# First sums of the down projection written by ScalarE, residual kept in the output, final sums added by GpSimd's DMAs

## The chip, the core and the metric

The kernel runs on one core of a Trainium2 chip. A core has TensorE (PE) for matrix products, VectorE (DVE) and ScalarE (ACT) for elementwise work, GpSimd (POOL) and SyncE (SP), each with its own queue of instructions that it works off in order. They meet only at semaphores: an instruction waits until those it depends on have reported. Data lies in the chip's DRAM, in on-chip SBUF of 128 partitions, and in PSUM, into which TensorE writes and from which VectorE and ScalarE read. DMA transfers between DRAM and SBUF are issued here by SP, later in part by GpSimd; 16 DMA engines carry them out. The metric is the device time of one execution in microseconds.

## The reference

One decoder block on 1024 tokens of width 1024. Two token mixers come first; what matters here is the end:

```python
        x = x + y @ w_out[l]
        xn2 = rmsnorm(x, norm2_g[l])
        x = x + jnp.square(jax.nn.relu(xn2 @ w_up[l])) @ w_down[l]
```

`w_up` is 1024 x 4096 and `w_down` is 4096 x 1024, all float32. The `x` of the first line, the residual, is needed twice: for the norm, and to be added to the result of the last line.

## The kernel before, in words

Every float32 operand is split into a high part and a low part (`split`, lines 318 to 320: ScalarE copies into the high part, VectorE subtracts it from the source for the low part), and a product is three matmuls: high by high, high by low, low by high. The large products use a scheme of seven instead of eight sub-products (N1 to N7), whose operands are sums of quarters of the matrices.

**Residual (lines 1040 to 1083).** For each of eight row blocks and two column halves TensorE forms `y @ w_out`, VectorE adds x, and SP stores the sum in `y_d`, a DRAM tile (line 1075). In the second half the first half of a row block is read back from `y_d` for the norm (line 1052).

**Up projection (`product`, `result`, `put_operand`).** Sixteen column units; the squared ReLU is turned into the operands of the down projection, split and stored in the DRAM tile `h_d` (line 1130, `h_d<-hs`).

**Down projection (`down`, lines 1155 to 1181).** The work is 32 blocks u = (c, t): eight chunks c of 512 of the 4096 hidden columns, and within each chunk four t; a block works on the row blocks t and t + 4. A block takes seven products of six 128x512 matmuls. Its rows of `h_d` come as two loads, `xh` and `xl` (`load_rows`, line 1146), into one of three places that rotate with u. The products go to three PSUM banks of a block:

- "a" (a tile `mm`): N1, which ScalarE copies with its sign turned into bank "b" (line 1172), then N2 on top of it;
- "b" (a tile `ms`): N6, N7, N4 one on top of the other;
- "d" (a tile `mm`): N5, then N3 on top of it.

After each product other than N1 VectorE adds or subtracts the bank into half of a row tile `Y[r]` of 128x1024 (line 1177). TensorE may put the next product on a bank only when the read before it is done: (u, N7) waits until N6's sum in "b" is read, (u, N4) until N7's is. `Y[0]` to `Y[7]` stay in SBUF over all chunks. They start from the residual: `load_sums` (line 1149) loads them from `y_d`, Y0 and Y4 early (line 1099), the other six when the up projection has ended (lines 1203 to 1205). In the last chunk SP stores each finished half to `out` (line 1179).

**Weights (class `Weights`).** Chunks of `w_down` come as four tiles `raw` (line 176), from which VectorE forms sums (line 153) and `split` makes the seven operands. Those of chunk 1 are called y1a, y1b, y1c, wh3/wl3, w1a, w1b and w1c, with h or l for the high and the low part.

**Order.** TensorE's order is written out by hand (main loop, lines 1216 to 1221): N6 and N5 of block u, N1 of u + 1, N7 of u, N2 of u + 1, N3 and N4 of u. The other engines' order is set by the scheduler of the framework from the order of the program and its own estimate of times. An instruction that waits holds up all that stands behind it on its engine.

Of the kernel before, what the change touches and what calls it, by code (L numbers as in the profile page):

```python
# [10 lines left out]
F = mybir.dt.float32  # L11
R = mybir.dt.float32r
AF = mybir.ActivationFunctionType
OP = mybir.AluOpType
# [255 lines left out]
def hybrid_block(ctx: ExitStack, tc: tile.TileContext, a: dict, out: bass.AP):  # L270
# [24 lines left out]
    v_d = dram.tile([HEADS, S, DH], F, name="v_d")  # L295

    h_d = dram.tile([FF // 512, 2, 4, P, 7, 2, P], F, name="h_d")
    y_d = dram.tile([S, D], F, name="y_d")

    def slot_of(from_):  # L300

# [699 lines left out]
    with ExitStack() as ph:  # L1001
# [41 lines left out]
        def load_rows(n):  # L1043

            nb, t = order[n]
            ts = slice(t * P, (t + 1) * P)
            xt = pn.tile([P, 512], F, name="xr")
            nc.sync.dma_start(xt, a["x"][ts, halves()[nb]])
            y0 = None
            if nb == 1:  # L1050
                y0 = pn.tile([P, 512], F, name="y0")
                nc.sync.dma_start(y0, y_d[ts, :512])
            ahead.append((xt, y0))

        load_rows(0)
        for nb in range(2):
            us = W.take(4)
            ns = halves()[nb]
            for n, t in enumerate([t for b, t in order if b == nb]):
# [12 lines left out]
                y = xt  # L1072
                nc.vector.tensor_tensor(y, pm, xt, op=OP.add)
                nc.scalar.activation(pm, y, AF.Square, accum_out=ssq[:, t, nb:nb + 1])
                nc.sync.dma_start(y_d[ts, ns], y)
                if nb == 1:
                    nc.vector.tensor_tensor(ssq[:, t, 2:3], ssq[:, t, 0:1], ssq[:, t, 1:2], op=OP.add)
                    rsqrt(ssq[:, t, 3:4], ssq[:, t, 2:3], 1.0 / D)
# [9 lines left out]
    with ExitStack() as ph:  # L1088
# [3 lines left out]
        def temps():  # L1092

            nonlocal up_pool
            if up_pool is None:
                assert pipe.slot > last_turn
                norm2.close()
                y0 = pool(sumst, "y0", 1)
                load_sums(0, [y0.tile([P, D], F, name=f"Y{r}") for r in (0, 4)])
                up_pool = pool(ph, "p26", 2)  # L1100
            return up_pool

# [43 lines left out]
                    nc.sync.dma_start(x.bitcast(F), h_d[c, i, t].rearrange("p o k q -> p (o k q)"))  # L1146
                    rows[u].append(x.rearrange("p (o k q) -> p o k q", o=7, k=2))

        def load_sums(t, places):

            for r, place in zip((t, t + 4), places):
                Y[r] = place
                nc.sync.dma_start(place, y_d[r * P:(r + 1) * P, :])

        def down(u, name):

            c, t = units[u]
            b = sums.setdefault(u, {})
            bank = BANK[name]
            fresh = bank not in b  # L1160
            if fresh:
                b[bank] = mm.tile([P, 512], F, name="mm")
            o = DOWN.index(name)
            wh, wl = W["dn", c, name]
            xh, xl = rows[u]
            pipe.step(b[bank], [(xh[:, o, k], xl[:, o, k], wh[:, 512 * k:512 * k + 512], wl[:, 512 * k:512 * k + 512])
                                for k in range(2)], None, fresh)
            ps = b[bank]
            lo, hi = halves()
            if name == "N1":  # L1170
                b["b"] = ms.tile([P, 512], F, name="ms")
                nc.scalar.activation(b["b"], ps, AF.Copy, scale=-1.0)  # L1172
            else:
                r, ns, op, last = {"N2": (t, lo, OP.add, True), "N6": (t, hi, OP.subtract, False),
                                   "N5": (t + 4, hi, OP.subtract, False), "N7": (t + 4, hi, OP.add, True),
                                   "N3": (t, hi, OP.add, True), "N4": (t + 4, lo, OP.add, True)}[name]
                nc.vector.tensor_tensor(Y[r][:, ns], Y[r][:, ns], ps, op=op)  # L1177
                if last and c == NC - 1:
                    nc.sync.dma_start(out[r * P:(r + 1) * P, ns], Y[r][:, ns])
            if t == 3:  # L1180
                W.free(("dn", c, name))

# [17 lines left out]
        exts.close()  # L1200
        y1 = pool(sumst, "y1", 1, "right")

        places = {t: [y1.tile([P, D], F, name=f"Y{r}") for r in (t, t + 4)] for t in (1, 3, 2)}
        for t in range(1, 4):
            load_sums(t, places[t])
        for x in "abc":
            W.places["y1" + x] = [y1.tile([P, UW], R, name=f"y1{x}{i}") for i in "hl"]
        W.free(("place", "y1"))
# [113 lines left out]
```

## Time and profile before

| | |
|---|---|
| median of 3 runs | 2300.4 us (2299.05 to 2302.49) |
| the profiled execution | 2299.8 us |
| its span, first to last instruction | 2297.7 us |
| PE matmul busy | 2236.2 us (97%) |
| DVE, ACT, POOL busy | 1341.9, 988.0, 103.0 us |
| SP's DMA queue | 351.63 MB, 48.3% of 16 engines |

The up projection's last units and the start of the down projection lie between about 1900 and 2015 us; the down projection then runs to the end. A row of the profile gives engine, source line, operation and output <- inputs; "L1177 DVE TENSOR_TENSOR Y<-Y,ms" is VectorE adding the bank "b" into Y. In rows of a timeline the first two numbers are start and duration in us, and a bracket gives the idle time before and what ended it. "SPq" rows are SP's issues of transfers, whose data lands later. In the table by stretch of time a DMA share near 1 means that all 16 engines are carrying data.

### The profile page before, as it was taken

To read this page: it belongs to the slowest core of one execution; us is meant where nothing else is said; L and a number is where in the kernel's file an instruction comes from. 1 tells how busy PE (TensorE), PEld (TensorE's weight loads), DVE (VectorE), ACT (ScalarE), POOL (GpSimd) and SP (SyncE) were. 2 spreads that over 40 slices of the span, in tenths; PEclk is the share of its full clock that TensorE was granted. 3 is DMA by queue.
4 is the path that set the end of the run, shared out by engine and by line. 5 is a ranking of instruction groups with operands and counts; after the bars stand their busy time and mean duration, and the time that the engine had idled before them with its cause. 6 is when DMAs were issued, how large, how long until landed. Compare 5 with 4: busy or idle time off the path is not lost.

```text
span 2297.7 us, 29975 instructions
## 1 busy us (share of the span) xinstructions
PE 2236.2 (97%) x10868; PEld 1915.5 (83%) x10868; DVE 1341.9 (58%) x2588; ACT 988.0 (43%) x2166; POOL 103.0 (4%) x148
## 2 busy tenths in 40 slices
PE   8999999999999999989999999999999999699999
PEld 7999999998888888878888778888787777588887
DVE  6444545455544445548777842453877778777774
ACT  5444435345443333435555533122666667422220
POOL 1111111110000000000000000000000000000000
PEclk9999999999999999999999999999999999899999
DMA  4313132223233333363433484554377789966655
GB/s 146 97 52 114 53 93 93 81 84 101 88 110 110 110 110 110 106 174 111 120 119 101 140 289 152 170 179 142 115 219 230 229 238 277 329 241 261 234 223 201
DMA packets 288805, 353.53 MB, mean 154 GB/s; under 512 B 14609, under 2 KB 215441, under 8 KB 288658
## 3 DMA queue, kind: packets, MB, share of 16 engines
q1 hardware_dynamic: 288658, 351.63, 48.3%
q8 instruction: 85, 1.39, 0.3%
q14 instruction: 62, 0.51, 0.1%
HBM read 229.84 MB, written 121.73 MB: 153 GB/s over the span
## 4 chain that ended last, share of the span: by engine, by line
PE 77%; DVE 8%; DMA 7%; ACT 4%; issue 3%; POOL 0%; SPq 0%; POOLq 0%; ACTq 0%; DVEq 0%
PE mm L223 51%; PE ms L223 20%; DMA raw<-in_w_up 3%; ACT wh L319 2%; DVE wl L320 2%; DMA h_d<-hs 1%; PE ms L605 1%; DVE hs L320 1%; PE ms L585 1%; DVE raw L121 1%; PE tr L661 1%; DVE xl L320 1%; PE ms L598 1%; PE ms L821 1%; DVE u L1120 1%
## 5 line engine op out<-in xcount | busy, mean ns | idle before, releaser
L223 PE MATMUL mm<-wh,xh 128*128 128x384 f32 (+1 forms) x1280 | 503.8, 394 | 0.0
L320 DVE TENSOR_TENSOR wl<-raw,wh 128x1024 fp32r<-128x1024 f32 (+2 forms) x274 | 297.4, 1088 | 298.6 <-ACT wh L319 295.5
L223 PE MATMUL mm<-wh,xl 128*128 128x384 f32 (+1 forms) x1280 | 460.4, 360 | 4.3 <-DVE xl L320 3.2
L223 PE MATMUL mm<-wl,xh 128*128 128x384 f32 (+1 forms) x1280 | 459.2, 359 | 0.0
L319 ACT ACTIVATE wh<-raw 128x1024 fp32r<-128x1024 f32 (+2 forms) x274 | 257.6, 949 | 301.0 <-PE mm L223 77.9
L223 PE MATMUL mm<-xl,wh 128*128 128x512 f32 x848 | 310.0, 390 | 1.7 <-DVE xl L320 1.7
L223 PE MATMUL mm<-xh,wh 128*128 128x512 f32 x848 | 310.5, 391 | 0.0
L223 PE MATMUL mm<-xh,wl 128*128 128x512 f32 x720 | 280.7, 390 | 0.0
L223 PEld LDWEIGHTS mm<-wh,xl 128*128 128x128 f32 x1280 | 241.4, 189 | 27.2 <-DVE xl L320 4.3
L223 PEld LDWEIGHTS mm<-wh,xh 128*128 128x128 f32 x1280 | 242.6, 190 | 21.0 <-ACT ms L1172 0.5
L223 PEld LDWEIGHTS mm<-wl,xh 128*128 128x128 f32 x1280 | 243.4, 190 | 19.1
L223 PE MATMUL ms<-xh,wh 128*128 128x512 f32 x604 | 239.8, 397 | 16.8 <-ACT u L393 13.8
L223 PE MATMUL ms<-xh,wl 128*128 128x512 f32 x604 | 236.0, 391 | 0.0
L223 PE MATMUL ms<-xl,wh 128*128 128x512 f32 x604 | 235.9, 391 | 0.0
L223 PEld LDWEIGHTS mm<-xl,wh 128*128 128x128 f32 x848 | 159.7, 188 | 35.1 <-DVE xl L320 2.1
L223 PEld LDWEIGHTS mm<-xh,wh 128*128 128x128 f32 x848 | 159.7, 188 | 34.0 <-ACT u L396 0.7
L223 PEld LDWEIGHTS mm<-xh,wl 128*128 128x128 f32 x720 | 135.6, 188 | 28.2
L223 PEld LDWEIGHTS ms<-xh,wh 128*128 128x128 f32 x604 | 113.8, 188 | 45.1 <-ACT u L393 18.8
L223 PEld LDWEIGHTS ms<-xh,wl 128*128 128x128 f32 x604 | 113.7, 188 | 24.0
L223 PEld LDWEIGHTS ms<-xl,wh 128*128 128x128 f32 x604 | 113.8, 188 | 22.3
L592 ACT ACTIVATE pr<-s,acc 128x128 f32<-128x128 f32 (+1 forms) x96 | 43.1, 449 | 148.4 <-DVE acc L590 125.5
L1177 DVE TENSOR_TENSOR Y<-Y,ms 128x512 f32<-128x512 f32 x96 | 65.8, 685 | 62.2 <-PE ms L223 62.1
(254 smaller groups left out, 3284.2 us busy)
## 6 DMA issues: line engine op xcount, KB each, us to landing
h_d<-hs SPq DMA_DIRECT2D x112, 512.0 KB, 5.7
xh<-h_d SPq DMA_DIRECT2D x32, 896.0 KB, 5.9
xl<-h_d SPq DMA_DIRECT2D x32, 896.0 KB, 7.2
raw<-in_w_att SPq DMA_DIRECT2D x48, 384.0 KB, 4.0
raw<-in_w_up SPq DMA_DIRECT2D x32, 512.0 KB, 5.1
raw<-in_w_down SPq DMA_DIRECT2D x32, 512.0 KB, 6.0
sg_d<-sg SPq DMA_DIRECT2D x32, 256.0 KB, 2.1
raw<-in_w_rqk_q SPq DMA_DIRECT2D x16, 512.0 KB, 3.7
```

Of the source, the lines that this page charges most:

```text
L121: self.nc.vector.tensor_tensor(x, x, y, op=OP.add)
L223: self.nc.tensor.matmul(ps, x, y, start=start, stop=stop, skip_group_check=not first)
L319: nc.scalar.activation(dst_h, src, AF.Copy)
L320: nc.vector.tensor_tensor(dst_l, src, dst_h.bitcast(F), op=OP.subtract)
L585: nc.tensor.matmul(sp[:, :n], qT[:, b * P:(b + 1) * P], kT[:, k0:k0 + n], start=True, stop=True)
L592: nc.scalar.activation(st["p"][:, :n], s[:, :n], AF.Exp, bias=acc[:, b, DH:DH + 1], accum_out=acc[:, b, DH + 1:DH + 2])
L598: nc.tensor.transpose(tp[:, j * P:(j + 1) * P], st["p"][:, j * P:(j + 1) * P], ident)
L605: nc.tensor.matmul(po[:, :DH], st["t"][:, j * P:(j + 1) * P], V[:, k0 // P + j, :], start=(j == 0), stop=(j == nk - 1))
L661: nc.tensor.transpose(pt[:, j, :], qk[:, j, :], ident)
L821: nc.tensor.matmul(sp[:, :P], kT[:, f], qT[:, f], start=(f == 0), stop=(f == 1))
L1120: nc.vector.tensor_tensor(held[j, x], held[j, x], held[j, y], op=OP.add)
L1177: nc.vector.tensor_tensor(Y[r][:, ns], Y[r][:, ns], ps, op=op)
```

## The change

The residual is stored in `out` itself instead of `y_d`, and read back from there for the norm. The eight loads of Y are gone: Y starts as the first sum of chunk 0. In each half of a row tile the first product that reaches it (N2, N6, N5 and N4 of chunk 0) is written by ScalarE, with the sign as its scale; N7 and N3 of chunk 0 and everything of later chunks are added by VectorE as before. At the end each finished half of Y is sent by GpSimd with a DMA that adds it to what is in `out`.

```diff
-    y_d = dram.tile([S, D], F, name="y_d")
...
-                nc.sync.dma_start(y0, y_d[ts, :512])
+                nc.sync.dma_start(y0, out[ts, :512])
...
-                nc.sync.dma_start(y_d[ts, ns], y)
+                nc.sync.dma_start(out[ts, ns], y)
...
-                load_sums(0, [y0.tile([P, D], F, name=f"Y{r}") for r in (0, 4)])
+                Y.update({r: y0.tile([P, D], F, name=f"Y{r}") for r in (0, 4)})
...
-        def load_sums(t, places):
-
-            for r, place in zip((t, t + 4), places):
-                Y[r] = place
-                nc.sync.dma_start(place, y_d[r * P:(r + 1) * P, :])
...
-                nc.vector.tensor_tensor(Y[r][:, ns], Y[r][:, ns], ps, op=op)
+                begun = c > 0 or name in ("N7", "N3")
+                if not begun:
+                    nc.scalar.activation(Y[r][:, ns], ps, AF.Copy, scale=1.0 if op == OP.add else -1.0)
+                else:
+                    nc.vector.tensor_tensor(Y[r][:, ns], Y[r][:, ns], ps, op=op)
                 if last and c == NC - 1:
-                    nc.sync.dma_start(out[r * P:(r + 1) * P, ns], Y[r][:, ns])
+                    nc.gpsimd.dma_start(out[r * P:(r + 1) * P, ns], Y[r][:, ns], accum_op=OP.add)
...
-        places = {t: [y1.tile([P, D], F, name=f"Y{r}") for r in (t, t + 4)] for t in (1, 3, 2)}
-        for t in range(1, 4):
-            load_sums(t, places[t])
+        Y.update({r: y1.tile([P, D], F, name=f"Y{r}") for t in (1, 3, 2) for r in (t, t + 4)})
```

TensorE's order of matmuls stays as it is. The other engines' orders move around the first blocks of the down projection. Three places follow, each with the rows of the program before and then of the changed one. The number behind a tile's name is that of its buffer; line numbers of the changed program are a few lower, apart from 1172, which is the copy of N1 before and the write of a first sum after.

On **VectorE**, where chunk 1's weights are made, before. Bank "b" of block 1 is ms_17791, and its N6 sum is the last row but one.

```order
L320 TENSOR_TENSOR y1bl_17728<-raw1_17703,y1bh_17727 128x1024
L320 TENSOR_TENSOR y1cl_17730<-raw2_17705,y1ch_17729 128x1024
L153 TENSOR_TENSOR raw0_17624<-raw0_17624,raw3_17707 128x1024
L1177 TENSOR_TENSOR Y1_17713<-Y1_17713,mm_17784 128x512
L153 TENSOR_TENSOR raw3_17707<-raw3_17707,raw2_17705 128x1024
L320 TENSOR_TENSOR wl3_17739<-raw0_17624,wh3_17738 128x1024
L153 TENSOR_TENSOR raw2_17705<-raw2_17705,raw0_17624 128x1024
L320 TENSOR_TENSOR w1al_17747<-raw3_17707,w1ah_17746 128x1024
L153 TENSOR_TENSOR raw1_17703<-raw1_17703,raw2_17705 128x1024
L320 TENSOR_TENSOR w1bl_17749<-raw2_17705,w1bh_17748 128x1024
L1177 TENSOR_TENSOR Y1_17713<-Y1_17713,ms_17791 128x512
L320 TENSOR_TENSOR w1cl_17751<-raw1_17703,w1ch_17750 128x1024
```

The same place in the changed program, where block 1's bank "b" is ms_17782 and block 2's is ms_17836:

```order
L1174 TENSOR_TENSOR Y5_17711<-Y5_17711,ms_17782 128x512
L1174 TENSOR_TENSOR Y1_17710<-Y1_17710,mm_17821 128x512
L319 TENSOR_TENSOR y1bl_17719<-raw1_17700,y1bh_17718 128x1024
L319 TENSOR_TENSOR y1cl_17721<-raw2_17702,y1ch_17720 128x1024
L153 TENSOR_TENSOR raw0_17621<-raw0_17621,raw3_17704 128x1024
L153 TENSOR_TENSOR raw3_17704<-raw3_17704,raw2_17702 128x1024
L319 TENSOR_TENSOR wl3_17730<-raw0_17621,wh3_17729 128x1024
L153 TENSOR_TENSOR raw2_17702<-raw2_17702,raw0_17621 128x1024
L319 TENSOR_TENSOR w1al_17738<-raw3_17704,w1ah_17737 128x1024
L153 TENSOR_TENSOR raw1_17700<-raw1_17700,raw2_17702 128x1024
L319 TENSOR_TENSOR w1bl_17740<-raw2_17702,w1bh_17739 128x1024
L1174 TENSOR_TENSOR Y6_17715<-Y6_17715,ms_17836 128x512
```

Block 1's N6 and N2 sums have left VectorE, its N7 and N3 sums stand ahead of the weights of chunk 1, and what now stands behind w1bl is block 2's N7 sum.

On **ScalarE** at the same place, before: ms_17791 and ms_17845 are the copies of N1 of blocks 1 and 2; that of block 3 comes after w1bh and w1ch.

```order
L1172 ACTIVATE ms_17791<-mm_17784 128x512
L319 ACTIVATE hs_17661<-q11_17524 128x512
L319 ACTIVATE hs_17689<-q12_17686 128x512
L319 ACTIVATE y1ah_17725<-raw0_17624 128x1024
L319 ACTIVATE hs_17694<-q12_17686 128x512
L1172 ACTIVATE ms_17845<-mm_17838 128x512
L319 ACTIVATE y1bh_17727<-raw1_17703 128x1024
L319 ACTIVATE y1ch_17729<-raw2_17705 128x1024
L319 ACTIVATE wh3_17738<-raw0_17624 128x1024
L319 ACTIVATE w1ah_17746<-raw3_17707 128x1024
L319 ACTIVATE w1bh_17748<-raw2_17705 128x1024
```

In the changed program, from the read of block 1's N6 (first row) to w1bh; the copy of block 3's N1 is the row after the last:

```order
L1172 ACTIVATE Y1_17710<-ms_17782 128x512
L1172 ACTIVATE Y5_17711<-mm_17821 128x512
L1165 ACTIVATE ms_17836<-mm_17829 128x512
L1172 ACTIVATE Y2_17714<-mm_17829 128x512
L318 ACTIVATE y1bh_17718<-raw1_17700 128x1024
L318 ACTIVATE y1ch_17720<-raw2_17702 128x1024
L1172 ACTIVATE Y5_17711<-ms_17782 128x512
L1172 ACTIVATE Y2_17714<-ms_17836 128x512
L1172 ACTIVATE Y6_17715<-mm_17875 128x512
L318 ACTIVATE wh3_17729<-raw0_17621 128x1024
L318 ACTIVATE w1ah_17737<-raw3_17704 128x1024
L318 ACTIVATE w1bh_17739<-raw2_17702 128x1024
```

Reads of the sums of blocks 1 and 2 now stand between and ahead of the weight splits, and the copy of block 3's N1 comes right behind w1bh, ahead of w1ch.

On **SP**, where the up projection's last rows have been stored, before: Y1 to Y7 are the loads of the residual, xh_91 and xl_92 the rows of block 3.

```order
L176 DMA raw3_17707<-in_w_down 128x1024
L1153 DMA Y1_17713<-y_d_90 128x1024
L1153 DMA Y5_17714<-y_d_90 128x1024
L1153 DMA Y2_17717<-y_d_90 128x1024
L1153 DMA Y6_17718<-y_d_90 128x1024
L1153 DMA Y3_17715<-y_d_90 128x1024
L1153 DMA Y7_17716<-y_d_90 128x1024
L176 DMA raw0_17758<-in_w_down 128x1024
L176 DMA raw2_17765<-in_w_down 128x1024
L176 DMA raw3_17767<-in_w_down 128x1024
L176 DMA raw1_17763<-in_w_down 128x1024
L1146 DMA xh_91<-h_d_89 128x1792
```

In the changed program, with xh_90 and xl_91 for block 3 and xh_94 and xl_95 for block 4:

```order
L176 DMA raw3_17704<-in_w_down 128x1024
L1145 DMA xh_90<-h_d_89 128x1792
L1145 DMA xl_91<-h_d_89 128x1792
L1145 DMA xh_94<-h_d_89 128x1792
L176 DMA raw0_17749<-in_w_down 128x1024
L176 DMA raw3_17758<-in_w_down 128x1024
L176 DMA raw2_17756<-in_w_down 128x1024
L176 DMA raw1_17754<-in_w_down 128x1024
L1145 DMA xl_95<-h_d_89 128x1792
```

The loads of block 3's rows have moved up from behind four loads of chunk 2's weights to directly behind those of chunk 1, and the load of block 4's xl stands behind the four.

## The prediction

> **What bounds the kernel now.** I read the clock and busy times by stretch first, then TensorE's own waits, then VectorE's order of time around the longest of them. Matmuls fill 97% of the span, so only a place where TensorE stands still can give time back. In the table by stretch the columns are the length, then PE, PEld, DVE, ACT and POOL busy with their counts, the granted clock, the DMA share and GB/s.
>
> ```profile
> 1960.00:1972.00 12.00, 11.88 (x52) 9.15 (x50) 11.20 (x15) 7.72 (x14) 0.00 (x0) 1.00 1.05 345
> 1972.00:1986.00 14.00, 11.26 (x42) 8.86 (x42) 8.48 (x13) 3.87 (x7) 0.00 (x0) 0.88 1.08 330
> 1986.00:2001.00 15.00, 0.00 (x0) 0.00 (x0) 11.25 (x11) 6.64 (x7) 0.00 (x0) 0.56 0.93 352
> 2001.00:2014.00 13.00, 11.58 (x43) 9.15 (x44) 6.20 (x9) 0.00 (x0) 0.00 (x0) 0.85 0.91 345
> 2014.00:2290.00 276.00, 276.00 (x1215) 227.21 (x1214) 188.57 (x240) 60.32 (x71) 0.00 (x0) 1.00 0.63 233
> ```
>
> From 2014 on TensorE never stops, so a microsecond saved before it ends the kernel a microsecond sooner. From 1986 to 2001 it does nothing. Here are its waits between 1920 and 2020: total, times, longest.
>
> ```profile
> PE ms L223 <- DVE Y L1177: 18.2, 2, 15.7
> PE ms L223 <- ACT u L393: 3.5, 1, 3.5
> PE mm L223 <- DMA xl<-h_d: 1.0, 1, 1.0
> ```
>
> Both waits of the first row are for a VectorE addition into Y that reads bank "b": N7 may not accumulate there until N6's sum is read. I write (u,Nk) for product k of block u; the waiting ones are (0,N7) and (1,N7). VectorE in order of time shows why the second is 15.7 us long:
>
> ```profile
> 1981.64 0.69 DVE L1177 TENSOR_TENSOR Y<-Y,ms 128x512 f32<-128x512 f32 x1
> 1989.65 1.23 DVE L320 TENSOR_TENSOR y1bl<-raw,y1bh 128x1024 fp32r<-128x1024 f32 x1 [7.33 <-ACT y1bh L319]
> 1990.97 1.23 DVE L320 TENSOR_TENSOR y1cl<-raw,y1ch 128x1024 fp32r<-128x1024 f32 x1
> ...
> 1998.39 1.22 DVE L153 TENSOR_TENSOR raw<-raw,raw 128x1024 f32<-128x1024 f32 x1
> 1999.53 1.22 DVE L320 TENSOR_TENSOR w1bl<-raw,w1bh 128x1024 fp32r<-128x1024 f32 x1
> 2000.66 0.68 DVE L1177 TENSOR_TENSOR Y<-Y,ms 128x512 f32<-128x512 f32 x1
> ```
>
> The addition at 2000.66, with which the stop ends, stands behind the weight work of chunk 1, which first waits 7.33 us for its weights and then takes 1.14 us a step (1998.39 to 1999.53). In the chain of waits the two stops also carry a slow start:
>
> ```profile
> 1974.42 2.93 PE ms L223 x6
> 2003.40 9.47 DMA xl<-h_d
> 2014.10 1.37 PE ms L223 x6
> ```
>
> Six matmuls take 1.37 us as a rule and 2.93 after the 2.50 us stop at 1974.42: **1.5 us lost to the clock** per such stop. The row at 2014.10 is (2,N7); from there the chain is matmuls to the end, so I carry everything to (2,N7).
>
> **The change, part by part.** *Sixteen first sums to ScalarE.* One costs VectorE 0.68 (the row at 2000.66) and ScalarE 0.58 us:
>
> ```profile
> L1172 ACT ACTIVATE ms<-mm x32: 580/582/584, 1962.8 to 2281.7; 128x512 f32<-128x512 f32 x32
> 1972.27 0.58 ACT L1172 ACTIVATE ms<-mm 128x512 f32<-128x512 f32 x1
> 1974.86 1.04 ACT L319 ACTIVATE y1ah<-raw 128x1024 fp32r<-128x1024 f32 x1
> 1978.12 0.63 ACT L319 ACTIVATE hs<-q 128x512 fp32r<-128x512 f32 x1 [2.21 <-DMA h_d<-hs]
> ```
>
> ScalarE is 3.87 of 14 us busy from 1972 to 1986, so the time fits. What counts is the queue: by the order of the changed program, the read of (0,N6) takes the place of the copy at 1972.27, and that of (1,N6) stands ahead of y1bh and y1ch, behind only the hs split that waits for a transfer until 1978.12.
>
> (0,N7) then starts at 1972.27 + 0.58, about 1972.9, instead of 1974.42, after a stop of 1.0 us. After one of 1.28 us the second matmul followed within 0.34, so I charge no slow clock:
>
> ```profile
> 1901.53 0.50 PE L223 MATMUL ms<-xh,wh 128*128 128x512 f32 x1 [1.28 <-ACT u L393]
> 1901.87 0.39 PE L223 MATMUL ms<-xl,wh 128*128 128x512 f32 x1
> ```
>
> *What is late next* are transfers and weights. Issues of SP, with the length of the issue and, below, KB and us to landing:
>
> ```profile
> 1976.71 1.72 SPq L1146 DMA_DIRECT2D xl<-h_d  x1
> 1982.01 3.16 SPq L176 DMA_DIRECT2D raw<-in_w_down  x3
> 1985.22 3.66 SPq L1153 DMA_DIRECT2D Y<-y_d  x6
> 2008.52 0.32 SPq L1146 DMA_DIRECT2D xh<-h_d  x1
> 2008.93 0.38 SPq L1146 DMA_DIRECT2D xl<-h_d  x1
> ...
> xl<-h_d SPq DMA_DIRECT2D x1, 896.0 KB, 7.5
> raw<-in_w_down SPq DMA_DIRECT2D x1, 512.0 KB, 6.4
> Y<-y_d SPq DMA_DIRECT2D x1, 512.0 KB, 10.4
> xh<-h_d SPq DMA_DIRECT2D x1, 896.0 KB, 6.5
> xl<-h_d SPq DMA_DIRECT2D x1, 896.0 KB, 8.3
> ```
>
> (a) (2,N1) is six products of 1.37 after (0,N7), at 1981.1; its third matmul, at 1981.6, needs the xl issued at 1976.71, which lands at 1984.2. That load hangs on transfers ahead of it, not on what changes. So a **new stop of 2.6** and 1.5 of slow clock. The first 3 us gained are lost again.
>
> (b) *The Y loads go.* The third raw (issued at about 1984.7) lands 6.4 later, at 1991.1, the last Y (issued at 1985.22 + 3.66 − 0.32 = 1988.56, plus 10.4) at 1998.9: six transfers at 1.3 each, **7.8 us of full queue**. Now xh and xl of block 3 stand directly behind raw. The pair at 2008.52 lands 2.2 apart (2015.0 and 2017.2), so block 3's rows land at 1991.1 + 4.4 = 1995.5 instead of 2012.9. TensorE: (2,N1) ends with the stop at 1984.2 + 0.9; (1,N7) ends at 1988.0 with the slow clock, then five products to 1994.8. (3,N1) asks for xl at 1995.25, waits 0.3 and ends at 1996.4. **(2,N7) starts at 1996.4 instead of 2014.1: 17.7 gained.**
>
> (c) *The weight work now hits ScalarE.* (3,N2) needs the copy of (3,N1), and that stands behind three weight splits (wh3, w1ah, w1bh), the first of them behind the read of (2,N5). TensorE ends (2,N5) at 1994.8, ScalarE reads it to 1995.4 and writes wh3 to 1996.4; VectorE needs 1.14 for its low part and 1.14 for the next raw sum (1998.7); w1bh then runs to 1999.8, the copy to 2000.4. (2,N7) ended at 1997.8: **a stop of 2.6 and 1.5 of slow clock**.
>
> (d) The rows of block 4 (its xl) now stand behind four raw loads, the last of which waits for w1cl: wl3 is done at 1997.6, then come five weight steps and one addition of 0.6, 6.3 us in all, to 2003.9. The xl goes out at 2004.4. The pair below, issued 0.41 apart in a quiet queue, took 6.3 for the second:
>
> ```profile
> xl<-h_d SPq DMA_DIRECT2D x1, 896.0 KB, 6.3
> ```
>
> With a raw of 512 KB ahead in place of an xh of 896 (0.9 less at 2.2 us for 896) it lands at 2009.8. TensorE, from 2000.4 with five products and the slow clock, asks at 2009.2: **a stop of 0.6**. After that the next rows are due 9.5 us apart as before, in a queue at 0.63.
>
> Sum at TensorE: 17.7 − 2.6 − 1.5 − 0.6 = **13.0 us**. Unknown are (a) to (d): with none of the stops from (0,N7) on, 17.7 + 2.6 + 1.5 + 0.3 = 22.1; with every stop of the list twice as long, 13.0 − 2.6 − 0.3 − 2.6 − 0.6 = 6.9. I keep 13.0, built from single rows.
>
> On the clock the Trainium skill says otherwise: "TensorE: Matmul & The Clock Gate", section "Why this matters for your kernels", has it that gaps up to about 3 us leave the clock alone. By it both new stops would lose nothing more, and the gain would be 3.0 larger. The trace does not agree: 2.50 us were enough.
>
> *The end.* The last addition and what leaves after it:
>
> ```profile
> 2293.98 0.69 DVE L1177 TENSOR_TENSOR Y<-Y,ms 128x512 f32<-128x512 f32 x1 [0.67 <-PE ms L223]
> out<-Y SPq DMA_DIRECT2D x16, 256.0 KB, 2.0
> y_d<-xr SPq DMA_DIRECT2D x16, 256.0 KB, 2.0
> y<-y_d SPq DMA_DIRECT2D x8, 256.0 KB, 2.7
> L333 POOL TENSOR_TENSOR ssq<-ssq,half 128x1 f32<-128x1 f32 x8 | 5.5, 690 | 309.5 <-DVE ssq L332 309.5
> ```
>
> The trace has no accumulating transfer and none from GpSimd. At least it is a write (2.0, as now: 0 lost, and nothing suggests less); at most a read and then a write, 2.7 + 2.0, with a GpSimd step of 0.7 ahead and another behind: 6.1, so 4.1 lost. I take the middle, **2.0 lost**. The other fifteen lie under matmuls.
>
> The Trainium skill, "DMA: Bandwidth & Descriptors", section "Anatomy of one DMA — SWDGE (gpsimd) path", gives about 2.0 us and bytes over 436 thousand for a plain transfer from GpSimd, 2.6 by my estimate for 256 KB; with it the end would lose 0.6 instead of 2.0. No run here shows it yet.
>
> *At nothing:* writing out instead of y_d keeps sizes and queue (the two rows of 256 KB). The two early Y loads have only matmuls beside them; without that cover they would be 2 × 1.3 us. SP's sixteen stores leave SP, where the last rows of h_d stood between them without a wait of TensorE. On GpSimd, by the order of the changed program, nothing else stands behind the sixteen transfers, so their waits hold nobody up.
>
> **Rivals.** All times are made comparable with the median, which is 0.6 above the profiled execution. *One: fewer stops.* TensorE's clock holds through 2.6 us, which gives 13.0 + 3.0 and 2286.4, or weights and rows come soon enough for no stop at all: 22.1 − 2.0, 2280.3. Against it: the 2.93 row, and rows that landed when (b) says. The first half is what the Trainium skill's page on the clock gate would have. *Two: more stops.* The weight work hits ScalarE's queue again, or rows come later, as the 9.47 us of the chain show they can: gain 6.9, end 4.1, 2297.6. *Three: the change does not do what it says.* ScalarE reads (1,N6) as late as VectorE did, and the stop only moves; then the 7.8 us of queue less the end are left, 2294.6, or nothing but the end, 2302.4. Against it: the read stands ahead of the weights. *Four: the accumulating transfers run one at a time in GpSimd's queue.* Sixteen leave from 2256.6 − 13.0 = 2243.6 on (the first store now is at 2256.6, the last lands at 2296.7):
>
> ```profile
> L1179 SPq DMA_DIRECT2D out<-Y x16: 332/332/383, 2256.6 to 2294.7; - x16
> ```
>
> At 3.3 us each they end at 2296.7, as before; from 3.6 on the kernel is slower by over 0.2%; at a read plus a write, 4.7, they end at 2318.8 and the kernel at 2322.5. For it: the read that each must make. Against it: SP's stores overlap, one every 1.37 us.
>
> **The numbers.** The profiled execution took 2299.8 around a span of 2297.7; 2299.8 − 13.0 + 2.0 = 2288.8, and 0.6 more for the median: **2289.4**. The forecast (2286.5 to 2293.5) has 0.62, rival one 0.13, two 0.12, three 0.06, four 0.07. A measurement of this kernel can tell about 0.2%, 4.6 us, from no change. Faster by more are the forecast, one, 0.08 of two and 0.03 of three: 0.86. Within it: 0.04 of two, 0.03 of three, 0.01 of four: 0.08. Slower: 0.06 of four. The range, 2283 to 2297, leaves out four, half of one, and a third of three and a few hundredths of two: 0.18.
>
> **What would show it.** TensorE's waits should have lost the 15.7 for VectorE's Y and show stops of 2 to 3 us at (2,N1) for an xl and at (3,N2) for ScalarE's ms, with the slow clock after both. Block 3's rows should land near 1995. ScalarE should read (1,N6) by 1981. The last GpSimd transfer should land 4 us after VectorE's last addition. Wrong is the forecast if a stop over 4 us is left, if a GpSimd transfer takes over 3 us each in turn, or if TensorE stops after 2014.

## The result, and the profile after

| | before | changed |
|---|---|---|
| median | 2300.41 us (6 runs, 2298.29 to 2302.49) | 2293.43 us (6 runs, 2292.53 to 2294.13) |
| span of the profiled execution | 2297.7 | 2291.8 |
| TensorE's last matmul ends | 2293.95 | 2283.96 |
| from there to the span's end | 3.8 | 7.9 |

The ratio is 0.997, with an interval of 0.9957 to 0.9983: 7.0 us less, where 11.0 were predicted. TensorE is done 10.0 us earlier, and 4.1 of these go again behind its last matmul.

TensorE's waits of the changed kernel between 1920 and 2060 (total, times, longest):

```profile
PE mm L223 <- DMA xl<-h_d: 8.7, 3, 4.5
PE mm L223 <- ACT ms L1165: 1.9, 2, 1.7
PE ms L223 <- ACT Y L1172: 0.8, 1, 0.8
```

The 15.7 us for VectorE's addition are gone, and new stops stand in their place. In TensorE's order of time they are these rows; in the bracket is the idle time and what ended it:

```profile
1969.89 0.50 PE L223 MATMUL ms<-xh 128*128 128x512 f32 x1 [0.79 <-ACT Y L1172]
1983.34 0.80 PE L223 MATMUL mm<-wh,xl 128*128 128x512 f32 x1 [4.52 <-DMA xl<-h_d]
1995.51 0.50 PE L223 MATMUL mm<-wh,xl 128*128 128x512 f32 x1 [0.89 <-DMA xl<-h_d]
1999.82 0.50 PE L223 MATMUL mm<-wh,xh 128*128 128x512 f32 x1 [1.74 <-ACT ms L1165]
2010.71 0.80 PE L223 MATMUL mm<-y1ah,xl 128*128 128x512 f32 x1 [3.32 <-DMA xl<-h_d]
```

They are (0,N7), block 2's xl at (2,N1), block 3's at (3,N1), the copy of (3,N1) at (3,N2), and block 4's xl at (4,N1). The second number is the duration of the matmul behind the stop: 0.80 where the granted clock has already fallen to half, as at the two long stops, and 0.50 at the others. The table by stretch, in the same five pieces as for before:

```profile
1960.00:1972.00 12.00, 11.21 (x50) 8.86 (x49) 9.90 (x13) 10.35 (x18) 0.00 (x0) 1.00 1.02 331
1972.00:1986.00 14.00, 9.48 (x37) 7.45 (x36) 4.37 (x7) 4.19 (x7) 0.00 (x0) 0.90 1.07 321
1986.00:2001.00 15.00, 12.37 (x52) 9.54 (x51) 11.23 (x11) 8.31 (x12) 0.00 (x0) 0.98 0.75 290
2001.00:2014.00 13.00, 9.68 (x37) 7.58 (x36) 8.91 (x9) 6.32 (x9) 0.00 (x0) 0.87 0.90 334
2014.00:2290.00 276.00, 269.77 (x1186) 221.61 (x1184) 181.37 (x231) 56.69 (x67) 14.10 (x16) 0.99 0.69 227
```

Where TensorE stood from 1986 to 2001, it now runs 52 matmuls, at a DMA share of 0.75 instead of 0.93. Before and behind that stretch it runs fewer than before (37 for 42, 37 for 43).

At the end, the last rows of the order of time:

```profile
2283.57 0.39 PE L223 MATMUL ms<-w1ch,xl 128*128 128x512 f32 x1
2283.99 0.69 DVE L1174 TENSOR_TENSOR Y<-Y,ms 128x512 f32<-128x512 f32 x1 [0.67 <-PE ms L223]
2285.08 0.87 POOL L1176 DMA_DIRECT2D out<-Y  x1 [0.50 <-DVE Y L1174]
```

And the group of the sixteen transfers (KB each, median us from issue to landing):

```profile
out<-Y POOLq DMA_DIRECT2D x16, 256.0 KB, 5.2
```

GpSimd is busy with each issue for 0.87 us and the data lands 5.2 after it, where SP's plain store took 2.0.

### The profile page after: what moved, and what is told of

Same layout as the page of the kernel before. It is cut to its first block, busy times and chain, and to the rows that moved or that the text cites. A ratio compares the mean times of both kernels' runs of the same rounds, so it can differ in the third digit from the quotient of the medians.

```text
span 2291.8 us, 29967 instructions
## 1 busy us (share of the span) xinstructions
PE 2234.7 (98%) x10868; PEld 1913.0 (83%) x10868; DVE 1332.1 (58%) x2572; ACT 995.9 (43%) x2182; POOL 117.1 (5%) x164
## 4 chain that ended last, share of the span: by engine, by line
PE 72%; DMA 9%; DVE 8%; ACT 5%; issue 4%; POOL 1%; SPq 0%; POOLq 0%; ACTq 0%; DVEq 0%
PE mm L223 49%; PE ms L223 18%; DMA raw<-in_w_up 2%; ACT wh L318 2%; DVE wl L319 2%; DMA h_d<-hs 2%; DVE raw L121 1%; PE ms L604 1%; PE ms L584 1%; DVE hs L319 1%; DMA xl<-h_d 1%; PE tr L660 1%; DMA raw<-in_w_gr_q 1%; DMA sr_d<-sg 1%; DVE xl L319 1%
## 5 line engine op out<-in xcount | busy, mean ns | idle before, releaser
L223 PE MATMUL ms<-xh,wh 128*128 128x512 f32 x604 | 240.1, 397 | 15.1 <-ACT u L392 11.3
L1174 DVE TENSOR_TENSOR Y<-Y,ms 128x512 f32<-128x512 f32 x88 | 60.3, 685 | 67.8 <-PE ms L223 67.8
```

The lines of the kernel that those rows point to most:

```text
L223: self.nc.tensor.matmul(ps, x, y, start=start, stop=stop, skip_group_check=not first)
```

## The experiments

After the first result two theories stood for the lost stop. **A:** the six Y loads made it: VectorE's additions needed them, and they stood in SP's queue ahead of block 3's rows; without them the stop goes, whoever writes the first sums. **B:** VectorE as the writer made it, since its additions stood behind the weight work; ScalarE's reads took it away. For the end, **C:** the accumulation makes the transfers longer; **D:** GpSimd's way of issuing does. Ratios are to the time before on the same chip; all comparisons of stretches come from the profiled executions.

### First sums by VectorE again, without the Y loads

```diff
-                    nc.scalar.activation(Y[r][:, ns], ps, AF.Copy, scale=1.0 if op == OP.add else -1.0)
+                    nc.vector.tensor_scalar(Y[r][:, ns], ps, 1.0 if op == OP.add else -1.0, None, op0=OP.mult)
```

> The changed kernel with the sixteen first sums written by VectorE instead of ScalarE; the loads of Y stay out. Theory A, the loads of Y made the 15.7 us stop (they filled the queue and their lateness put the reads behind the weight work): the stop does not come back, TensorE's stops stay at the blocks' xl loads and at the copy of block 3's N1, time 2293.4 within 2.5. Theory B, ScalarE made the difference by reading the banks while VectorE makes weights: a stop of over 10 us at (1,N7) comes back, time 2300 or more.

2285.25 us, 0.9959 (0.9945 to 0.9973), somewhat better than A expected. Its waits of TensorE between 1920 and 2060, the first four:

```profile
PE mm L223 <- DMA xl<-h_d: 4.9, 3, 1.8
PE ms L223 <- DVE Y L1172: 2.4, 1, 2.4
PE mm L223 <- ACT ms L1165: 1.6, 1, 1.6
PE ms L223 <- DVE Y L1174: 1.2, 1, 1.2
```

No stop is over 2.4 us, with VectorE as the writer. So B falls, and of A it holds that the stop goes with the loads. Which part of A made the stop, data that came late or the loads' place in SP's queue, this run can't tell. VectorE's reads of the first sums come at once here; no loaded Y is waited for, and the weight work now stands behind them in VectorE's order:

```profile
1973.65 0.69 DVE L1172 TENSOR_SCALAR Y<-ms 128x512 f32<-128x512 f32 x1
1975.01 0.69 DVE L1172 TENSOR_SCALAR Y<-ms 128x512 f32<-128x512 f32 x1 [0.67 <-PE ms L223]
```

### The same bytes back in SP's queue, ScalarE still the writer

```diff
+    y_c = dram.tile([2, 4, P, D], F, name="y_c")
...
+        for t in range(1, 4):
+            for i in range(2):
+                nc.sync.dma_start(y_c[i, t], h_d[NC - 1, i, t, :, 2:6].rearrange("p o k q -> p (o k q)"))
```

> The changed kernel with six transfers of 512 KB (copies from h_d to a spare DRAM tile) in the place where the six loads of Y stood on SP; nothing waits for their data. ScalarE still writes the first sums. Theory A: the rows of block 3 land 8 to 15 us later than 1995.5, TensorE stops there for as long, and the time goes back to 2298 to 2304. Theory B: (1,N7) is read by ScalarE in time, so the gain stays, 2293.4 within 2.

2305.84 us, 1.0049 (1.0034 to 1.0064), worse than expected. ScalarE reads the first sums in "b" as early as in the changed kernel, from 1977.66 on in its order of time. Then TensorE stands at block 3's rows (first the order of ScalarE, then TensorE's waits from 1950 to 2030, then SP's issues):

```profile
1977.66 0.60 ACT L1174 ACTIVATE Y<-ms 128x512 f32<-128x512 f32 x1 [0.16 <-PE ms L223]
1979.02 0.60 ACT L1174 ACTIVATE Y<-ms 128x512 f32<-128x512 f32 x1 [0.76 <-PE ms L223]
```

```profile
PE mm L223 <- DMA xh<-h_d: 17.6, 1, 17.6
```

```profile
1986.24 4.79 SPq L1205 DMA_DIRECT2D y_c<-h_d  x6
1998.12 5.39 SPq L176 DMA_DIRECT2D raw<-in_w_down  x4
2003.60 0.38 SPq L1147 DMA_DIRECT2D xh<-h_d  x1
```

So an early read alone is worth nothing: the stop moves from (1,N7) to (3,N1). The copies are not the only thing in the way, though. The scheduler also put four weight loads ahead of the rows, as in the kernel before; the changed kernel issues these rows ahead of the loads. The trace says which of the two sets the end of the stop. The last copy goes out at 1990.32 and takes this long (KB, us to landing); then SP waits for VectorE's weight work, which must free a buffer before the first of the four loads can go out:

```profile
y_c<-h_d SPq DMA_DIRECT2D x1, 512.0 KB, 8.6
```

```profile
SPq L176 <- DVE raw L153: 7.0, 1, 7.0
```

The copies have landed by 1998.9, and the rows go out only at 2003.60, behind the four loads. In the kernel before it is the same: the last Y lands at 1998.9, and block 3's rows go out at 2002.93. In the changed kernel they go out at 1984.33. So what delays the rows is the order on SP, in which they stand behind loads that wait; the bytes of the six transfers alone would have been through by then. The runs don't show the six transfers in this place with the rows ahead of the four loads.

### The same copies, later

```diff
             load_rows(u + 3)
+            if 8 <= u < 14:
+                i, t = u % 2, u // 2 - 3
+                nc.sync.dma_start(y_c[i, t], h_d[NC - 1, i, t, :, 2:6].rearrange("p o k q -> p (o k q)"))
```

> The changed kernel with the same six copies of 512 KB as in queue_back, but one behind the rows of each of blocks 8 to 13 of the down projection, where TensorE does not wait. If the place ahead of block 3's rows makes the copies dear: no stop there, the time of the changed kernel, 0.997 to 0.9985 of the time before, and the copies cost nothing. If six more transfers and their spare memory cost wherever they stand: over 1.000. It also tells what made the up projection longer (319 to 320 us from its first matmul to product 7 of block 0 in the three profiles with six more transfers behind it, 313.5 to 318 in the seven without, though the instructions up to there are in the same order): if more transfers in the program or the spare memory do it, about 320 here; if it hangs on their place, or is scatter, 313 to 318.

2290.22 us, 0.9973 (0.9963 to 0.9984): the time of the changed kernel, with no stop at block 3's rows. The six transfers are free where the queue has room. The stretch before (0,N7), "up" in the table below, took 315.6 us. That speaks against the number of transfers as what lengthens that stretch.

### The residual's place alone, and both kernels once more

The kernel before with `out` in place of `y_d` for the residual, all loads, additions and stores as they were:

```diff
-                nc.sync.dma_start(y_d[ts, ns], y)
+                nc.sync.dma_start(out[ts, ns], y)
...
-                nc.sync.dma_start(place, y_d[r * P:(r + 1) * P, :])
+                nc.sync.dma_start(place, out[r * P:(r + 1) * P, :])
```

> The kernel before with one edit: the residual is written to the output's memory and read back from there; the Y loads, the sums on VectorE and the plain stores stay. Both theories of the stop (A: the Y loads ahead of block 3's rows in SP's queue made it; B: VectorE as writer of the first sums made it) expect 1.000 of the time before, within 0.002, a stop of 15 to 16.5 us at block 2's product 7 or block 3's product 1, and an end of 2.8 us from the last matmul to the last landing. Where the place of the residual itself cost or gave something, it would be over 1.002 or under 0.998. The stretch of the up projection from its first matmul to product 7 of block 0 took 320 us in the profile before and 317 us in the changed one: if that is scatter of the raw loads' landings, this kernel gives anything from 316 to 320; if the change makes it, about 320.

2295.50 us, 1.000 (0.999 to 1.0009), and the stop is there, with its first row of TensorE's waits reading "18.4, 2, 15.9". The edit costs and gives nothing.

> The changed kernel, unaltered, beside the others on one chip: 0.997 (0.996 to 0.998) of the time before; stops of 4.5, 0.9, 1.7 and 3.3 us at block 2's product 1, block 3's products 1 and 2 and block 4's product 1, each within 1.5 us; from the last matmul to the last landing 6.5 us.

2289.66 us, 0.9982 (0.9972 to 0.9991), at the upper edge of what was expected. The stop at (3,N1) didn't come; the others were 4.6 at (2,N1), 2.7 at (3,N2) and 3.4 at (4,N1).

> The kernel before, unaltered, for a second profile: 1.000 within 0.001; the stop of 15 to 16.5 us; from the first matmul of the up projection to product 7 of block 0, 319 to 321 us if that stretch depends on the program, anything from 313 to 320 if it is scatter.

2294.66 us, 0.9998 (0.9988 to 1.0007). With these there are two profiles of each kernel. Up: from an early matmul of the up projection, the same in every kernel (the first that writes `ms` from `xl`, at 1651.56 in the profile before), to TensorE's arrival at (0,N7). Down: from there to the end of the last matmul. Tail: from there to the end of the span. Arrival is the start of the last matmul ahead of (0,N7), plus 0.23, the distance at which matmuls follow each other.

| | up | down | tail | down and tail |
|---|---|---|---|---|
| before | 320.2 | 322.2 | 3.8 | 326.0 |
| before_again | 314.9 | 323.0 | 3.8 | 326.8 |
| res_out | 319.1 | 322.8 | 3.8 | 326.5 |
| changed | 317.3 | 315.0 | 7.9 | 322.9 |
| changed_again | 313.5 | 318.7 | 7.5 | 326.2 |
| queue_late | 315.6 | 316.2 | 7.3 | 323.5 |
| queue_back | 320.2 | 326.3 | 7.9 | 334.2 |
| end_sp | 316.8 | 314.9 | 3.8 | 318.7 |
| end_pool_plain | 316.6 | 315.5 | 4.8 | 320.4 |
| first_dve | 316.0 | 312.4 | 7.3 | 319.7 |
| late_res | 318.1 | 313.6 | 3.8 | 317.3 |
| late_res_rows | 316.7 | 315.2 | 3.8 | 319.0 |
| dve_late | 316.9 | 310.9 | 3.8 | 314.7 |
| dve_late_rows | 317.5 | 314.9 | 3.8 | 318.7 |

The same kernel's up stretch differs by 5.3 us between two profiles of before and by 3.8 between two of the changed one, so the 2.9 us by which the changed kernel was ahead there in the first pair can be scatter. The right column averages 326.4 in the first three rows and 324.2 in the next three, whose down projection and end are those of the changed kernel: 2.2 us for the change, 3.1 between the first profiles of the two kernels and 0.6 between the second. The medians of these three kernels against the time before say 7.0, 5.8 and 4.8. The up stretch is 2.6 shorter on average in those same rows, and before_again's profiled execution was itself 2.4 below the median of its kernel. Whether the change also shortens the up projection by a microsecond or two, where queue_back has the same instructions in the same order up to there and took 320.2, these profiles can't tell: that part of the gain stays open.

The two profiles of the changed kernel differ by 3.7 us in "down" as well. In the second one the copy of (3,N1) held TensorE for 2.66 us, and the slow clock followed:

```profile
1993.70 0.50 PE L223 MATMUL mm<-wh,xh 128*128 128x512 f32 x1 [2.66 <-ACT ms L1165]
```

Yet the stops together are hardly longer than in the first. The table by stretch, over the 50 us from the arrival on, for the changed kernel, for changed_again and for first_dve:

```profile
1968.94:2018.94 50.00, 38.73 (x153) 30.36 (x153) 30.33 (x35) 24.02 (x35) 0.00 (x0) 0.93 0.83 286
1962.03:2012.03 50.00, 38.64 (x137) 29.88 (x137) 27.66 (x31) 22.85 (x33) 0.00 (x0) 0.83 0.85 283
1965.22:2015.22 50.00, 39.09 (x163) 29.90 (x163) 40.84 (x51) 16.95 (x21) 0.00 (x0) 1.00 0.85 292
```

TensorE stands still for 11.3, 11.4 and 10.9 us of the 50, but the granted clock is 0.93, 0.83 and 1.00 on average, and "down" follows it: 315.0, 318.7 and 312.4. So the difference between these three lies in the clock, not in how long TensorE waits. The last section shows what the clock goes by.

### The end: which part of it costs

Two kernels with other final stores, by SP and by GpSimd, both plain:

```diff
-                    nc.gpsimd.dma_start(out[r * P:(r + 1) * P, ns], Y[r][:, ns], accum_op=OP.add)
+                    nc.sync.dma_start(out[r * P:(r + 1) * P, ns], Y[r][:, ns])
```

> The changed kernel with its sixteen final transfers issued by SP as plain stores; the residual is left out of the output. In the profile of the changed kernel the last GpSimd transfer lands 6.5 us after the last matmul ends, before SP's landed 2.8 after it. If GpSimd's accumulating transfers cost the end 3.7 us, this run is 3.7 shorter than the changed kernel's 2293.4: 2289.7, with nothing moved before the last matmul. If the end is hidden or is the same for every transfer, 2293.4. If the transfers also disturbed the loads of the last rows, TensorE would end earlier too; I expect it does not.

2287.59 us, 0.9969 (0.9953 to 0.9985), where 3.7 us less than the changed kernel were expected.

```diff
-                    nc.gpsimd.dma_start(out[r * P:(r + 1) * P, ns], Y[r][:, ns], accum_op=OP.add)
+                    nc.gpsimd.dma_start(out[r * P:(r + 1) * P, ns], Y[r][:, ns])
```

> The changed kernel with the sixteen final transfers still issued by GpSimd but as plain stores; the residual is left out of the output. This splits the 5.4 us from issue to landing into the way over GpSimd and the accumulation. If the accumulation makes them long (a read of the destination before the write), they land about 3 us after issue and the run takes about 2291; if GpSimd's way of issuing does, they land 5 us after issue as with accumulation and the run takes 2293.4.

2288.09 us, 0.9967 (0.9956 to 0.9978). The group of the stores by SP (KB each, us to landing), then of those by GpSimd without accumulation, and GpSimd's own group for their issues (busy us, mean ns of one):

```profile
out<-Y SPq DMA_DIRECT2D x16, 256.0 KB, 2.0
```

```profile
out<-Y POOLq DMA_DIRECT2D x16, 256.0 KB, 2.3
```

```profile
L1176 POOL DMA_DIRECT2D out<-Y x16 | 8.9, 554 | 636.5 <-DVE Y L1174 629.0 <-DMA xl<-h_d 7.4
```

The tail is 3.8 with SP, 4.8 with plain stores by GpSimd and 7.9 with accumulation (7.3 to 7.9 in the five profiles that have it): of the 4.1 us that the end lost, 1.0 is GpSimd's way and 3.1 the accumulation. C explains most, D the rest. This rests on the tails. The times don't resolve it: both ratios agree within their intervals with the changed kernel's, 0.997 and 0.9982, and the changed kernel was not measured beside these two on their chip.

### The residual added earlier, on the chip

The residual's rows are loaded into weight buffers that come free, and VectorE adds them in blocks 27 to 30; SP stores plainly:

```diff
+            if u >= len(units) - 5 and u < len(units) - 1:
+                for r in (u - 27, u - 23):
+                    nc.vector.tensor_tensor(Y[r], Y[r], res[r].bitcast(F), op=OP.add)
...
+            for buf, t in {26: ((0, 0), (1, 1)), 27: ((2, 2), (5, 3))}.get(u, ()):
+                for r, x in zip((t, t + 4), W.buffer(buf)):
+                    res[r] = x
+                    nc.sync.dma_start(x.bitcast(F), out[r * P:(r + 1) * P, :])
```

> The changed kernel, but the output's residual is loaded by eight transfers into weight buffers that come free in blocks 26 and 27, added by VectorE in blocks 27 to 30 (8 adds of 128x1024; those of the split take 1.22 us each, so 2.4 us a block beside the 4.1 us of a block's six adds in 8.7 us), and the final sums are stored plainly by SP. If the accumulating transfers alone make the later end: the tail from the last matmul to the last landing goes from 6.5 back to 2.8 us and the rest after it from 1.4 to 1.0, so 4.1 us less than the changed kernel, about 0.9950 of the time before. If the adds or the loads hold TensorE up instead (rival): new waits for VectorE in the last five blocks, up to 8 x 1.2 = 9.8 us, and the time is that of the changed kernel or up to 0.999.

2286.31 us, 0.9965 (0.9954 to 0.9976), against 0.9982 for the changed kernel beside it: 3.4 us less, as the tail said (4.1). TensorE has no wait from 2230 on. VectorE's groups there show that the eight additions fit between its waits for TensorE; the last row has four of them, and a row like it the other four:

```profile
L1174 DVE TENSOR_TENSOR Y<-Y,ms 128x512 f32<-128x512 f32 x18 | 12.2, 685 | 9.8 <-PE ms L223 9.7
...
L1215 DVE TENSOR_TENSOR Y<-Y,wl 128x1024 f32<-128x1024 f32 x4 | 4.9, 1222 | 3.3 <-DMA wl<-out 3.3
```

The same with block 4's rows ahead of the weights of chunk 2 (raw loads are held back in class `Weights` until the rows are issued):

```diff
+    W.hold = len(W.src) + 8
...
+            if u == 1:
+                W.hold = 10 ** 6
+                while W.load():
+                    pass
```

> As the last kernel, and besides the raws of chunk 2 are held back on SP until block 4's rows are issued, as they are in the kernel before. If block 4's rows stand late for the four raws ahead of them, the 3.3 us stop at block 4's product 1 and about 1.5 us of slow clock behind it go: 4 to 5 us less than the last kernel, about 0.993 of the time before. Rival: the weights of chunk 2 come too late then or the stop moves to another product: the same time as the last kernel or more.

2286.11 us, 0.9962 (0.9948 to 0.9975): no gain. The stop at (4,N1), 2.8 in late_res, is gone. But a wait for VectorE's addition comes up later (1.30 at 2018.86) that wasn't there, and (3,N2) stands 2.33 us with the slow clock behind it, where late_res had 0.94 at (3,N1) and 1.66 at (3,N2) without it. So far the rival holds. Part of the loss need not be the edit's, though: the stop at (2,N1) was 4.46 instead of 2.87, because that load went out 1.6 us later after the arrival, and it scatters from profile to profile.

### First sums by VectorE and the residual late

Both edits on the changed kernel at once, the residual's as in late_res, and:

```diff
-                    nc.scalar.activation(Y[r][:, ns], ps, AF.Copy, scale=1.0 if op == OP.add else -1.0)
+                    nc.vector.tensor_scalar(Y[r][:, ns], ps, 1.0 if op == OP.add else -1.0, None, op0=OP.mult)
```

> late_res with the first sums written by VectorE, as in first_dve. If both gains add: late_res was 0.9965 and first_dve 1 to 3 us below the changed kernel, so 0.9952 to 0.996 of the time before; stops as in first_dve (2.6, 1.9, 1.6, 1.8, 1.9 us), a tail of 2.8 us and 1.0 behind it. Rival: the stops that were short with VectorE were so by scatter: 0.9965 as late_res.

2282.03 us, 0.9939 (0.9924 to 0.9955): **the best of all, 13.0 us under the time before**, and better than expected. The gains add, and "down" is the shortest of the table, 310.9. With late_res against it (0.9965) and first_dve against the changed kernel, VectorE as the writer of the first sums was 2 to 6 us the better one both times, though in both pairs the intervals overlap.

And the raws of chunk 2 held back besides:

```diff
+    W.hold = len(W.src) + 8
```

> dve_late, and the raws of chunk 2 held back until block 4's rows are issued. In late_res_rows this took the stop at block 4's product 1 away and lengthened others as much, so no difference from dve_late within 2 us; if the stop at block 4 is the last one that counts with VectorE, 2 to 4 us less.

2289.12 us, 0.9966 (0.9953 to 0.9979), 7 us worse where no difference was expected; in the profiles "down" is 4.0 longer. Block 4's rows now come in time, but VectorE does the held weight work in one stretch just when first sums and banks have to be read. Its order of time, and then TensorE's stop that ends with the last of these rows:

```profile
2016.53 1.22 DVE L154 TENSOR_TENSOR raw<-raw,raw 128x1024 f32<-128x1024 f32 x1
2017.66 0.68 DVE L1174 TENSOR_SCALAR Y<-ms 128x512 f32<-128x512 f32 x1
2018.26 1.21 DVE L154 TENSOR_TENSOR raw<-raw,raw 128x1024 f32<-128x1024 f32 x1
2019.40 1.22 DVE L320 TENSOR_TENSOR wl<-raw,wh 128x1024 fp32r<-128x1024 f32 x1
2020.53 0.68 DVE L1176 TENSOR_TENSOR Y<-Y,ms 128x512 f32<-128x512 f32 x1
```

```profile
2021.26 0.79 PE L224 MATMUL ms<-w1ah,xh 128*128 128x512 f32 x1 [3.88 <-DVE Y L1176]
```

## Why the prediction was near, and where it failed

The time fell as forecast and came out 4.0 us above the figure, inside the range. Much of that nearness is luck: the first profile of the changed kernel is 2.8 us ahead when the down projection starts, and in the six profiles averaged above the down projection and the end together gave only 2.2 us. To compare without it, here are the prediction's points counted from TensorE's arrival at (0,N7), which is the start of (0,N7) less its idle time: 1974.42 − 2.50 = 1971.92 before, 1969.89 − 0.79 = 1969.10 after.

| us from the arrival | before | predicted | changed |
|---|---|---|---|
| (0,N7) starts | 2.5 | 1.0 | 0.8 |
| block 2's xl read at (2,N1) | 12.7 | 12.3 | 14.2 |
| block 3's xl landed | 41.0 | 23.6 | 26.4 |
| (3,N2) starts | 43.4 | 28.5 | 30.7 |
| block 4's xl read at (4,N1) | 50.7 | 37.9 | 41.6 |
| last matmul ends | 322.0 | 309.0 | 314.9 |

- **(0,N7) and its clock:** right, 0.79 us for 1.0 and no slow clock.
- **(a):** the stop at (2,N1) and the slow clock came, but 4.5 long for 2.6. The xl went out 6.3 us after the arrival (1975.40) instead of 4.8 (1976.71) and took 7.9 for 7.5. The step took that issue as given by the transfers ahead of it and not touched by the change. This issue scatters: by the table's count of the arrival it came 4.5 to 6.6 us behind it in the eight profiles with ScalarE's sums and 4.3 to 5.3 in the six with VectorE's, so one profile was too little to take it to the tenth. Why it scatters was not tried.
- **(b):** the mechanism is shown: the loads' going lets block 3's rows out early. Of the 17.4 us that the landing was to gain, 14.6 came; 1.8 of the 2.8 that lack were lost before the third raw had landed, about as much as (a)'s load went out late. What the step didn't credit right is ScalarE: first_dve shows that its reads weren't needed, and queue_back that they don't help alone. And of the loads it counts the 7.8 us of queue, where the trace of queue_back shows that the order on SP, with the rows behind four waiting weight loads, is what holds them longest.
- **(c):** the stop at (3,N2) was there for the reason given, ScalarE's copy behind three weight splits. It was 1.74 us without the slow clock in one profile, after 0.89 at (3,N1), and 2.66 with it in the other; 2.6 and 1.5 were predicted.
- **(d) failed in size:** 3.3 us and the slow clock instead of 0.6 without it. The landing was late by 3.7 on this count: 2.1 from the issue, which followed the late weight work, and 1.5 from the transfer, which took 6.9 and not 5.4. The quiet queue of the quoted pair was the wrong row for it: the DMA share was 0.90 here. In the chain of waits the transfer stands with its 6.94, and the four matmuls behind it with 2.08 instead of the 0.91 that four take at full clock:

```profile
2003.73 6.94 DMA xl<-h_d
2010.71 2.08 PE mm L223 x4
```

- **The end failed in size:** 4.1 lost, the upper bound, for the middle of 2.0. A transfer that reads and then writes came out at 5.2 us, above 2.7 + 2.0, and GpSimd's issue at 0.87.
- **The clock:** the prediction charged 1.5 us for a stop of 2.5 and nothing for one of 1.28. The price was right, 1.6 behind (a). The rule was not: the length of a stop doesn't decide, as the last section shows, so that (c) had the slow clock in one profile and not in the other.
- **Its own signs:** the one against it, "if a stop over 4 us is left", came true with the 4.52 at (2,N1), and the last transfer landed 5.8 us after VectorE's last addition instead of 4. The other signs came as written: block 3's rows landed at 1995.5, ScalarE read (1,N6) at 1978, and TensorE has no wait over 0.2 us after 2014.
- **The rivals:** four did not come; the sixteen transfers overlap, since the one issued at 2283.73 is followed by the next at 2285.08 with landings 5 us behind. Two came in part, as (d). One did not come. Three did not come as written, since ScalarE's reads were early, as the change says; but it was not they that took the stop away.
- **The pages of the Trainium skill:** by "DMA: Bandwidth & Descriptors", section "Anatomy of one DMA — SWDGE (gpsimd) path", a plain transfer from GpSimd was 2.6 by estimate; 2.3 was measured. The page has nothing by which 5.2 could be told. On "TensorE: Matmul & The Clock Gate", section "Why this matters for your kernels", which leaves gaps of up to about 3 us without effect, the runs disagree, as the last section shows.

So from the predicted 13.0 at TensorE 7.1 remained by this count (322.0 − 314.9); the end took 4.1, and the rest of the measured 5.9 us of span is what the up projection was ahead.

## What to carry to other kernels

Where a reader is late because of what it waits for, moving the read to another engine doesn't help; count what stands ahead of its data in the queue of transfers, and what those transfers wait for in their turn. A load that nothing needs for long goes to a place where the queue has room: here six transfers right at the start of the down projection, with the order that the scheduler then chose, cost 10 us (334.2 against 324.2 from the arrival to the end), and nothing from its ninth block on. An accumulating transfer as the very last step of a kernel is dear, and the same addition in an idle slot of VectorE some blocks earlier was free.

## What the runs showed of the hardware

An accumulating DMA of 256 KB took 4.7 to 5.2 us from issue to landing (medians of five profiles) and 0.87 us of GpSimd, without accumulation 2.3 and 0.55; SP's store took 2.0.

The slow clock doesn't follow from a stop's length alone. In end_sp it came behind a stop of 1.86 us, in end_pool_plain it stayed away behind one of 2.94. TensorE's rows behind these two stops:

```profile
1996.67 0.50 PE L223 MATMUL mm<-wh,xh 128*128 128x512 f32 x1 [1.86 <-ACT ms L1165]
```

```profile
1998.56 0.50 PE L223 MATMUL mm<-wh,xh 128*128 128x512 f32 x1 [2.94 <-ACT ms L1165]
```

This speaks against a fixed limit near 3 us, as the Trainium skill's page "TensorE: Matmul & The Clock Gate" has it in the section "Why this matters for your kernels": a shorter stop was followed by the slow clock and a longer one was not. The granted clock in the traces shows what decides. In every profile it changes only at the edges of windows of 3.41 us, which follow each other on one grid wherever the stops lie. Here are three such windows in a row around each stop, in the columns of the prediction's table, first of end_sp and then of end_pool_plain:

```profile
1991.35:1994.76 3.41, 2.64 (x11) 1.80 (x10) 3.11 (x3) 2.20 (x3) 0.00 (x0) 1.00 0.31 126
1994.76:1998.17 3.41, 1.55 (x7) 1.23 (x7) 3.41 (x4) 2.41 (x3) 0.00 (x0) 1.00 0.51 166
1998.17:2001.58 3.41, 3.41 (x9) 2.63 (x8) 2.57 (x5) 1.73 (x3) 0.00 (x0) 0.50 0.88 281
```

```profile
1993.56:1996.97 3.41, 2.07 (x10) 1.37 (x8) 3.11 (x4) 1.88 (x3) 0.00 (x0) 1.00 0.07 26
1996.97:2000.38 3.41, 1.82 (x8) 1.51 (x9) 3.41 (x4) 2.73 (x4) 0.00 (x0) 1.00 0.68 198
2000.38:2003.79 3.41, 3.41 (x17) 2.81 (x16) 3.38 (x4) 2.02 (x3) 0.00 (x0) 1.00 0.81 279
```

In end_sp the whole stop falls into one window, which has TensorE idle for 1.86 us, and the next window runs at half clock. In end_pool_plain the edge at 1996.97 cuts the longer stop into 1.34 and 1.59 us, and the clock stays. All fourteen profiles agree between 1655 and 2280 us: each of the 48 windows at full clock with more than 1.85 us idle was followed by one at half clock, and none of the 2437 with less than 1.75 us was; between the two it went either way. Behind a window at half clock the full clock came back where TensorE had been idle for at most 0.5 us of it, and not where it had been idle for 0.86 or more.

So it counts how much of a stop falls into one window. Where the edges fall differs from one execution to the next: the first window at half clock begins 14.2 us after the arrival in the first profile of the changed kernel and 12.4 in the second. A window at half clock costs up to half its length, 1.7 us, and the second profile has five of them where the first has two. Several short stops are better than one long one of the same sum, as first_dve shows with 10.9 us of stops and no window at half clock; there is luck in it, since an edge cut its longest, of 2.42 us, in two.
